# Late steps of a hybrid decoder kernel moved, and its paged key scores spread into the next stage

## The chip, the cores and the metric

The kernel runs on one core of one Trainium2 chip. The metric is device time in microseconds (us). The kernel before takes 2168.29 us, the median of three runs (2164.63 to 2173.03).

## The reference, cut to what matters

One layer of a decoder works on a prompt (1024 tokens behind 16 learned meta tokens) and on a sample batch (8 sequences of 4 new tokens, each with 1024 past tokens in a paged cache). Everything is in 32-bit floating point.

```python
h = rms_norm(x, norm_pre_g)
(q, k, v), sg, (gq, gk, gv, gf), gg = branch_inputs(h, w_in, w_alpha, b_alpha)   # h @ w_in, split
o_sb  = sb_prompt(q, k, v, sb_bias)          # or sb_sample(...) with past keys and values by page_table
o_gla = gla_prompt(gq, gk, gv, gf)           # or one gla_chunk from state_gla
mixed = concat([o_sb * silu(sg), rms_norm(o_gla) * silu(gg)])
x = x + rms_norm(mixed @ w_out, norm_post_g)
```

`w_in` is 2048 x 7184 and `w_out` 2048 x 2048. The stick-breaking attention has 8 heads of 128: the weight of a key is exp(log_sigmoid(z) - the sum of softplus(z) over all later keys). The gated linear attention has 4 heads with keys of 128 and values of 256, and its decay comes from a rank of 16 (`w_alpha`). For the samples the scores of the past keys are needed: 8 sequences x 8 pages x 8 heads = 512 blocks of 128 keys, each against 4 queries.

## The kernel before, in words

All 1072 tokens (16 + 1024 + 32) stay on chip as hT, 16 tiles of 128 features, each split into a high part `hh` and a low part `hl`. `inproj` (L279) makes one block of 128 output columns: it loads the weights 256 rows at a time (`weight_chunk`, L177: one DMA on SyncE's queue, the high part cast on ScalarE, L184, the low part subtracted on VectorE, L185), and does three matmuls (high x high, high x low, low x high; L289 to L291) for each of 16 row blocks and three chunks of tokens, into three PSUM buffers `acc`. A projection is 8 weight chunks x 3 token chunks = 24 steps of six matmuls.

The order of the work is laid out by hand. `Weaver` (L51) holds a heap of Python generators, each due at a certain beat. After each of the 24 steps `inproj` calls `W.beat()`, which lets every generator that is due record its next piece; `yield n` makes it due n beats later. One beat is called a unit here. `flush` calls the beat until no generator is left but those spawned as `lasting`; `drain` until none at all is left. Beats of a flush or a drain have no projection in them. A scheduler then sets the final order on each engine from what was recorded; pieces under `urgent()` (weights, evictions of `acc`) go ahead.

The stages are these:
- The first heads' loads and norms, then 8 attention heads (`head`, V, K and Q projections), the low-rank product of the decay (`low_rank`, L297: the load `war`, the split into `wa` on ScalarE and VectorE, then 96 matmuls into `acc_ga`), and the gate projections 0 to 2.
- The gated linear attention (pool `gp`): for each of 4 heads the projections gk, gq and two of gv. `decay` (L709) loads `w_alpha` six times into 16 rows each, and for each chunk of tokens loads `ga`, does one matmul `al` (L723) and goes on to the cumulated decay `cb`. `own` (L741) makes the diagonal products P_d (L747, L753), three of them into two PSUM buffers, each multiplied by the identity on VectorE (L749, L754). `level` does seven further steps. `inside` (L794) runs `own` and the levels, then the end of the keys: `packed` (L829: a copy into `rep` on VectorE, a transpose on TensorE) and `by_token` (L839: transposes, L845, into kd). `chunks` (L888) starts when kd is there. `samples_out` (L872) scales two tiles on VectorE (L876), and transposes them (L882) three units later. Gate projections 3 and 4 follow.
- The paged stage (pool `dp`): the weights of the samples from the scores (`new_keys` L1077, `chain` L1092), the value pages (`vr`, 64 loads of 512 KB), and gate projections 5 to 13.
- The output product by seven block products: gates 14 and 15, then `step` with `weights` (L1270) for `w_out`.

**The paged keys.** `z_feed` (L344) is a lasting generator. For each page it does four products on VectorE (L379), one per query: the key page `kp` (64 KB, three buffers) times the query row `qb`, summed into a column of `zt`. It loads two pages ahead. A finished `zt` goes to memory (`zd`, L384), from where `chain` fetches it in the paged stage, once all heads of that sequence are through (`z_done`). Each page is due two units after the one before. All its tiles are in the pool `dk`, which the tiles of `weight_forms` (L395) share; `dk` closes before the paged stage, and the drain at L999 ahead of that runs the feed to its end.

SyncE issues nearly all DMAs, in order: weights, pages, states and outputs stand in one queue. The staging tiles (`stage`, 128 x 384) come from one pool `stg` of seven buffers. `W.mark` ties the first product of a page, by an order without a semaphore, behind the last projection matmul recorded.

Of the kernel before, what the change touches and what calls it, by code (L numbers as in the profile page):

```python
# [20 lines left out]
P = 128  # L21
# [29 lines left out]
class Weaver:  # L51
# [25 lines left out]
    def drain(self):  # L77
        while self.heap:
            self.beat()
# [3 lines left out]
def hybrid_step(ctx: ExitStack, tc: tile.TileContext, x_prompt, x_sample, cache_k, cache_v, state_gla,  # L83
# [213 lines left out]
    def low_rank():  # L297

        war = stage("war")
        warv = war[:, :256].rearrange("p (k c) -> p k c", c=16)  # L300
        nc.sync.dma_start(warv, w_in[0, :, C_GA:C_GA + 16].rearrange("(k p) c -> p k c", p=P))
        wa = [stg.tile([P, 8, 32], F32R, tag="stg", name=f"wa{i}") for i in range(2)]
        for i in range(2):
            act.copy(wa[i][:, :, 0:16], warv[:, 8 * i:8 * i + 8])
            vec.tensor_tensor(wa[i][:, :, 16:32], warv[:, 8 * i:8 * i + 8], wa[i][:, :, 0:16].bitcast(F32), ALU.subtract)
        acc = [accp.tile([P, 512], F32, tag="acc", name=f"acc_ga_{c}") for c in range(3)]
# [15 lines left out]

    dk_cm = tc.tile_pool(name="dk", bufs=2, side="right")
# [20 lines left out]
    def z_feed(rate):  # L344
# [8 lines left out]
        def fetch(h, b, i):  # L353
            if i == 0:
                qbs[h, b] = dk.tile([P, NT, P], F32, tag="qb", bufs=2, name=f"qb{b}_{h}")
                nc.sync.dma_start(qbs[h, b][:], qsd[b * NT:(b + 1) * NT, h * P:(h + 1) * P].partition_broadcast(P))
            kps[h, b, i] = dk.tile([P, P], F32, tag="kp", bufs=3, name=f"kp{b}_{h}_{i}")
# [5 lines left out]
        for n, (h, b, i) in enumerate(pages()):  # L363
# [10 lines left out]
            if i == 0:  # L374
                zt = dk.tile([P, NT, NPG], F32, tag="zt", name=f"zt{b}_{h}")
            kp = kps.pop((h, b, i))
            for t in range(NT):
                jk = dk.tile([P, P], F32, tag="jk", bufs=1, name=f"jk{b}_{h}_{i}_{t}")
# [60 lines left out]
    with tc.tile_pool(name="sp", bufs=1) as sp, tc.tile_pool(name="sps", bufs=1, space=PSUM) as sps:  # L439
# [195 lines left out]
    with tc.tile_pool(name="gp", bufs=1) as gp, tc.tile_pool(name="gps", bufs=1, space=PSUM) as gps:  # L635
# [73 lines left out]
        def decay(g, cb):  # L709

            raw = stage(f"walr{g}")[:96, :P]
            for i in range(6):
                nc.sync.dma_start(raw[16 * i:16 * i + 16], w_alpha[0, :, g * P:(g + 1) * P])
            wal = gp.tile([96, P], F32R, tag="wal", name=f"wal{g}")
            act.copy(wal[:], raw)
            vec.tensor_tensor(wal[64:96, :], raw[64:96], wal[64:96, :].bitcast(F32), ALU.subtract)
            for c, (lo, hi) in enumerate(CHUNKS):
                n = hi - lo
                ga = stg.tile([96, 384], F32R, tag="stg", name=f"ga{g}_{c}")
                nc.sync.dma_start(ga[:, :n].bitcast(F32), gad[:, lo:hi])  # L720
                yield 5
                ps = gps.tile([P, 512], F32, tag="P", bufs=2, name=f"al{g}_{c}")
# [18 lines left out]
        def own(g, at, kt, qt):  # L741

            for c0 in (0, EB):
                ps = gps.tile([P, 512], F32, tag="P", bufs=2, name=f"P{g}_d_{c0}")
                for i in range(4):
# [4 lines left out]
                                  ident[:].unsqueeze(1).to_broadcast([P, 4, P]), ALU.mult)  # L750
            ps = gps.tile([P, 512], F32, tag="P", bufs=2, name=f"P{g}_d_8")
# [42 lines left out]
        def inside(g, at, kt, qt, cb, res):  # L794

            own(g, at, kt, qt)
# [24 lines left out]
            packed(kt[:, REAL:T], pk[:], 2, f"k{g}")  # L821
# [7 lines left out]
        def packed(src, dst, lo, nm):  # L829
# [681 lines left out]
```

## Time and profile before

| What | us |
|---|---|
| median of three runs | 2168.29 |
| profiled execution | 2170.9 |
| its span | 2169.2 |
| TensorE busy (PE) | 2083.5 |
| VectorE busy (DVE) | 1571.3 |
| ScalarE busy (ACT) | 989.6 |
| mean granted clock of TensorE | 0.989 |

A page of the profile gives busy times by engine, groups of instructions by source line (L379 is line 379 of the kernel), and DMA queues. Views of the trace add: who waited for whom (waits), busy time in chosen windows with the granted share of TensorE's clock, and instructions in order of time (timeline). PE is the matmuls, PEld the loads of their stationary operand, SPq the queue of SyncE. Matmuls overlap in the records: one of 384 columns is shown with some 330 ns, and they follow each other at about half of that.

### The profile page before, as it was taken

What the parts mean: (1) busy time and instruction counts of PE and PEld (TensorE: products, weight loads), DVE (VectorE), ACT (ScalarE), POOL (GpSimd) and SP (SyncE); (2) the same over time, 40 slices, a digit from 0 to 9 for tenths busy, and PEclk for the clock granted to TensorE, in tenths of its full rate; (3) what the DMA queues carried; (4) which work ended last, traced back from release to release, by engine and by line L of the source; (5) the groups of instructions that cost most, each with busy time, mean ns of one, the idle gap of its engine ahead of it and who ended that gap; (6) DMA issues with size and microseconds to landing.
All of it is one profiled execution on the core that took longest, in us unless ns stands there. A gap on an engine that the chain in (4) does not pass through costs nothing.

```text
span 2169.2 us, 43319 instructions
## 1 busy us (share of the span) xinstructions
PE 2083.5 (96%) x12546; PEld 1877.2 (87%) x12546; DVE 1571.3 (72%) x6592; ACT 989.6 (46%) x2536; POOL 83.7 (4%) x298
## 2 busy tenths in 40 slices
PE   5999999999999999989999999999999999999997
PEld 5999999999999979889899898998888897777765
DVE  6368889888898889788887888877544337453575
ACT  7345546565555646323535335243443335342332
POOL 0000010100001010010000000000000000000000
PEclk9999999999999999999999999999999999999998
DMA  6225554555545444423333433334776666452484
GB/s 194 54 72 135 143 152 138 154 154 138 165 140 158 139 126 119 133 76 81 104 99 86 113 81 106 94 84 136 221 232 219 222 200 201 130 157 73 129 277 172
DMA packets 380803, 304.02 MB, mean 140 GB/s; under 512 B 50771, under 2 KB 321043, under 8 KB 380563
## 3 DMA queue, kind: packets, MB, share of 16 engines
q1 hardware_dynamic: 378370, 300.97, 47.5%
q8 instruction: 99, 1.62, 0.3%
q14 instruction: 142, 1.16, 0.2%
q10 hardware_dynamic: 2192, 0.27, 0.1%
HBM read 243.39 MB, written 57.72 MB: 139 GB/s over the span
## 4 chain that ended last, share of the span: by engine, by line
PE 67%; DVE 14%; DMA 11%; ACT 3%; issue 3%; SPq 1%; POOL 0%; DVEq 0%; ACTq 0%; POOLq 0%
DVE jk L379 5%; DMA kp<-in_cache_k_dram 5%; PE acc_g L289 4%; PE acc_g L291 4%; PE acc_g L290 4%; PE b L1420 4%; PE b L1421 4%; PE b L1422 3%; PE acc_k L289 3%; PE acc_k L290 3%; PE acc_k L291 3%; PE acc_gv L289 2%; PE acc_gv L291 2%; PE acc_gv L290 2%; PE acc_q L289 2%
## 5 line engine op out<-in xcount | busy, mean ns | idle before, releaser
L379 DVE SCALAR_TENSOR_TENSOR jk<-kp,qb 128x128 f32<-128x128 f32 x2048 | 590.9, 289 | 93.4 <-DMA kp<-in_cache_k_dram 54.0
L289 PE MATMUL acc_g<-hT,wh_g 128*128 128x384 f32 (+2 forms) x768 | 253.8, 330 | 1.4 <-ACT gx L433 1.1
L291 PE MATMUL acc_g<-hT,wl_g 128*128 128x304 f32 (+2 forms) x768 | 248.1, 323 | 0.4 <-DVE wl_g L185 0.4
L290 PE MATMUL acc_g<-hT,wh_g 128*128 128x304 f32 (+2 forms) x768 | 247.9, 323 | 0.0
L1420 PE MATMUL b<-ring,f 128*128 128x512 f32 x416 | 166.4, 402 | 7.3 <-ACT gx L433 3.5
L289 PEld LDWEIGHTS acc_g<-hT,wh_g 128*128 128x128 f32 x768 | 145.0, 189 | 27.0 <-ACT wh_g L184 13.4
L1284 DVE TENSOR_TENSOR ring<-wr,ring 128x512 fp32r<-128x512 f32 x104 | 70.7, 690 | 132.0 <-ACT ring L1283 131.7
L379 DVE DVE_READ_ACCUMULATOR jk<-kp,qb 128x1 f32 x2048 | 166.1, 81 | 0.0
L1421 PE MATMUL b<-ring,f 128*128 128x512 f32 x416 | 163.1, 392 | 1.0 <-DVE ring L1284 1.0
L1422 PE MATMUL b<-ring,f 128*128 128x512 f32 x416 | 162.8, 391 | 0.0
L291 PEld LDWEIGHTS acc_g<-hT,wl_g 128*128 128x128 f32 x768 | 144.9, 189 | 2.6 <-issue 1.9
L290 PEld LDWEIGHTS acc_g<-hT,wh_g 128*128 128x128 f32 x768 | 145.0, 189 | 0.7
L1283 ACT CAST ring<-wr 128x512 fp32r<-128x512 f32 x104 | 64.0, 621 | 161.4 <-DMA wr<-in_w_out_dram 79.8
L507 ACT ACTIVATE X<-X 127x512 f32<-127x512 f32 (+4 forms) x112 | 54.9, 491 | 166.5 <-DVE X L506 166.3
L289 PE MATMUL acc_gv<-hT,wh_gv 128*128 128x384 f32 (+1 forms) x384 | 129.9, 338 | 0.0
L289 PE MATMUL acc_k<-hT,wh_k 128*128 128x378 f32 (+1 forms) x384 | 127.6, 332 | 0.0
L291 PE MATMUL acc_gv<-hT,wl_gv 128*128 128x384 f32 (+1 forms) x384 | 126.5, 329 | 0.0
L290 PE MATMUL acc_gv<-hT,wh_gv 128*128 128x384 f32 (+1 forms) x384 | 126.2, 329 | 0.0
L290 PE MATMUL acc_k<-hT,wh_k 128*128 128x378 f32 (+1 forms) x384 | 125.4, 326 | 0.0
L289 PE MATMUL acc_q<-hT,wh_q 128*128 128x368 f32 (+2 forms) x384 | 125.3, 326 | 0.0
L291 PE MATMUL acc_k<-hT,wl_k 128*128 128x378 f32 (+1 forms) x384 | 125.2, 326 | 0.0
L290 PE MATMUL acc_q<-hT,wh_q 128*128 128x368 f32 (+2 forms) x384 | 123.6, 322 | 0.0
(427 smaller groups left out, 5488.1 us busy)
## 6 DMA issues: line engine op xcount, KB each, us to landing
kp<-in_cache_k_dram SPq DMA_DIRECT2D x512, 64.0 KB
vr<-in_cache_v_dram SPq DMA_DIRECT2D x64, 512.0 KB
qb<-qsd SPq DMA_DIRECT2D x64, 256.0 KB
tf<-in_w_out_dram SPq DMA_DIRECT2D x64, 256.0 KB
td<-tf SPq DMA_DIRECT2D x64, 256.0 KB
wr_g<-in_w_in_dram SPq DMA_DIRECT2D x128, 128.0 KB
wr<-td SPq DMA_DIRECT2D x64, 256.0 KB
wr<-in_w_out_dram SPq DMA_DIRECT2D x48, 256.0 KB
```

Source lines behind the costliest of these rows:

```text
L289: mm(acc[c][:, :n], wh[:, k2, :], hh[k][:, lo:hi], start=(k == 0), stop=False)
L290: mm(acc[c][:, :n], wh[:, k2, :], hl[k][:, lo:hi], start=False, stop=False)
L291: W.mark = mm(acc[c][:, :n], wl[:, k2, :], hh[k][:, lo:hi], start=False, stop=(k == NK - 1)).ins
L379: ins = vec.scalar_tensor_tensor(jk[:], kp[:], 1.0, qbs[h, b][:, t, :], ALU.mult, ALU.mult, accum_out=zt[:, t, NPG - 1 - i:NPG - i])
L507: act.activation(X, X, AF.Exp)
L1283: act.copy(wh, r)
L1284: vec.tensor_tensor(wl, r, wh.bitcast(F32), ALU.subtract)
L1420: mm(bk[:], ah, wh, start=first and k == 0, stop=False, skip_group_check=True)
L1421: mm(bk[:], ah, wl, start=False, stop=False, skip_group_check=True)
L1422: mm(bk[:], al, wh, start=False, stop=last and k == 7, skip_group_check=True)
```

## The change

It has two parts. The first moves instructions in the recorded order:
- the load of `war` and the split into `wa` become a generator of their own, due 58 units after the start of the last head, that is within its Q projection (`low_rank_weights`);
- `decay` waits six units between the load of `w_alpha` and its cast, and loads each chunk's `ga` ahead of the chunk that uses it;
- `own` yields three units after each of its two large products;
- the copies into `rep` are made ahead of a wait instead of just before the transpose, and the wait for the keys grows from 5 to 7 units;
- `samples_out` waits nine units instead of three;
- `new_keys` waits 10 and 2 units instead of 2 and 10;
- the first four tiles of `w_out` are loaded before gate projection 15.

The second part concerns the paged keys: every sixth page is due three units after the one before instead of two (13/6 units per page on average); the tiles of `z_feed` are in a pool `zq` of their own, which closes after the paged stage; the drain at the end of the gated stage leaves one generator, the feed, on the heap; and the paged stage ends with a drain instead of a flush.

```diff
-    def drain(self):
-        while self.heap:
+    def drain(self, keep=0):
+        while len(self.heap) > keep:
             self.beat()
...
-    def low_rank():
+    wa = []
+    def low_rank_weights():
         war = stage("war")
...
         nc.sync.dma_start(warv, w_in[0, :, C_GA:C_GA + 16].rearrange("(k p) c -> p k c", p=P))
-        wa = [stg.tile([P, 8, 32], F32R, tag="stg", name=f"wa{i}") for i in range(2)]
+        yield 6
+        wa.extend(stg.tile([P, 8, 32], F32R, tag="stg", name=f"wa{i}") for i in range(2))
...
+    zq_cm = tc.tile_pool(name="zq", bufs=2, side="right")
+    zq = zq_cm.__enter__()
     dk_cm = tc.tile_pool(name="dk", bufs=2, side="right")
...
-        W.spawn(z_feed(lambda n: 2), lasting=True)
+        W.spawn(z_feed(lambda n: 2 + (n % 6 == 5)), lasting=True)
...
         for h in range(HEADS):
+            if h == HEADS - 1:
+                W.spawn(low_rank_weights(), 58)
             head(h)
...
+            def load_ga(c):
+                lo, hi = CHUNKS[c]
+                gas[c] = stg.tile([96, 384], F32R, tag="stg", name=f"ga{g}_{c}")
+                nc.sync.dma_start(gas[c][:, :hi - lo].bitcast(F32), gad[:, lo:hi])
+
+            load_ga(0)
+            yield 6
             wal = gp.tile([96, P], F32R, tag="wal", name=f"wal{g}")
...
                 yield 5
+                ga = gas.pop(c)
+                if c < 2:
+                    load_ga(c + 1)
...
                 vec.tensor_tensor(at[:, j:j + 4, :], ps[:].rearrange("p (a t) -> p a t", t=P),
                                   ident[:].unsqueeze(1).to_broadcast([P, 4, P]), ALU.mult)
+                yield 3
...
-            own(g, at, kt, qt)
+            yield from own(g, at, kt, qt)
...
-            yield 5
+            rep_ = three(kt[:, REAL:T], f"k{g}")
+            yield 7
...
             for i in range(2):
                 vec.tensor_scalar(ow[i], ow[i], r[:, i:i + 1], None, ALU.mult)
-            yield 3
+            yield 9
...
-        W.drain()
+        W.drain(1)
...
         def new_keys():
-            yield 2
+            yield 10
...
-            yield 10
+            yield 2
...
-        W.flush()
+        W.drain()
+    zq_cm.__exit__(None, None, None)
...
+        firsts = []
+        for k in range(4):
+            firsts.append(oy.tile([P, 512], F32, tag="wr", name=f"wr10_{k}")[:])
+            spread(nc.sync.dma_start(firsts[k], w_out[0, P * k:P * (k + 1), 0:512]))
         gate_group(15)
```

In `z_feed` the tiles qb, kp, zt and jk change their pool from `dk` to `zq`; in `gv_tok` the copy `three(...)` moves ahead of `yield 2`; `weights` takes its first four tiles from `firsts`.

More of the change, by code (lines that the diff above doesn't have):

```diff
@@ L817, in inside @@
             vec.tensor_tensor(kt[:, :T], kt[:, :T], ke[:, :T], ALU.mult)
-            yield 5
+            rep_ = three(kt[:, REAL:T], f"k{g}")
+            yield 7
             kd = xtile(f"kd{g}")
             pk = gp.tile([96, P], F32R, tag="pk", name=f"pk{g}")
-            packed(kt[:, REAL:T], pk[:], 2, f"k{g}")
+            packed(rep_, pk[:], 2, f"k{g}")
             by_token(kt, kd, (0, 4), col, f"k{g}")
@@ L827, in inside, with three, packed @@
             res["kd"], res["ebl"], res["pk"] = kd, ebl, pk
-        def packed(src, dst, lo, nm):
-            ps = gps.tile([P, 512], F32, tag="tr", name=f"trp_{nm}")
+        def three(src, nm):
             rep = stage(f"rep_{nm}")[:, :96]
             vec.tensor_copy(rep.rearrange("p (a t) -> p a t", a=3), src.unsqueeze(1).to_broadcast([P, 3, NSMP]))
+            return rep
+        def packed(rep, dst, lo, nm):
+            ps = gps.tile([P, 512], F32, tag="tr", name=f"trp_{nm}")
             nc.tensor.transpose(ps[:96, :P], rep, ident[:])
@@ L852, in gv_tok @@
         def gv_tok(g, f, c, lo, raw, v, pv):
+            if c == 2:
+                rep = three(raw[:, REAL - lo:T - lo], f"v{g}_{f}")
             yield 2
@@ L855, in gv_tok @@
             if c == 2:
-                packed(raw[:, REAL - lo:T - lo], pv[:, f * P:(f + 1) * P], 1, f"v{g}_{f}")
+                packed(rep, pv[:, f * P:(f + 1) * P], 1, f"v{g}_{f}")
         def chunk_out(g, c, rows, ow, ssq):
```

27 lines of the change are left out of this document (15 added, 12 removed).

## The prediction

> **What bounds the kernel now.** I read the page first. The span and the busy line say that TensorE (PE) is the engine to follow:
>
> ```profile
> span 2169.2 us, 43319 instructions
> ...
> PE 2083.5 (96%) x12546; PEld 1877.2 (87%) x12546; DVE 1571.3 (72%) x6592; ACT 989.6 (46%) x2536; POOL 83.7 (4%) x298
> ```
>
> PE is idle for 2169.2 - 2083.5 = 85.7 us. The change adds and removes no matmul, so it can only win idle time of PE, and time in which PE runs at a lower clock. Next comes the view of PE's waits, in which the idle time has names:
>
> ```profile
> PE otr_s L882 <- DVE ow_s L876: 7.1, 4, 2.9
> PE P_d L753 <- DVE at L749: 6.6, 3, 5.6
> ...
> PE acc_ga L310 <- DVE q L616: 3.6, 1, 3.6
> PE b L1420 <- ACT gx L433: 3.5, 2, 3.0
> PE al L723 <- DMA kp<-in_cache_k_dram: 3.4, 1, 3.4
> ...
> PE Cs L1080 <- issue: 2.7, 1, 2.7
> PE tr_k L845 <- DVE pk L837: 2.7, 4, 0.8
> ...
> PE acc_gk L289 <- ACT gx L433: 1.9, 1, 1.9
> ```
>
> The columns are the total in us, the number of waits and the longest. All are single waits at seams of the recorded order, not a steady shortage. The third view is busy time and granted clock in short windows around the larger of them:
>
> ```profile
> 786.00:796.00 10.00, 6.62 (x35) 3.95 (x36) 8.95 (x43) 4.33 (x15) 0.21 (x1) 0.83 0.62 191
> 898.00:908.00 10.00, 8.14 (x41) 7.82 (x40) 5.85 (x30) 3.77 (x10) 0.00 (x0) 0.83 0.48 141
> 912.00:932.00 20.00, 15.39 (x77) 14.86 (x76) 13.71 (x74) 6.54 (x15) 9.96 (x34) 0.83 0.40 101
> 964.00:976.00 12.00, 8.28 (x35) 8.19 (x36) 8.94 (x44) 0.81 (x2) 0.00 (x0) 0.72 0.26 67
> 1090.00:1098.00 8.00, 5.83 (x38) 5.38 (x37) 5.27 (x36) 1.63 (x7) 0.00 (x0) 1.00 0.31 83
> 1224.00:1232.00 8.00, 6.20 (x40) 5.75 (x39) 4.88 (x35) 1.59 (x7) 0.00 (x0) 1.00 0.41 109
> 1360.00:1368.00 8.00, 5.21 (x24) 5.12 (x25) 5.12 (x35) 1.57 (x6) 0.00 (x0) 0.79 0.22 55
> 1522.00:1536.00 14.00, 11.26 (x51) 9.97 (x51) 9.77 (x29) 8.30 (x21) 0.00 (x0) 0.76 0.71 214
> 1812.00:1822.00 10.00, 6.60 (x20) 4.54 (x21) 10.00 (x21) 5.89 (x13) 0.11 (x1) 0.83 0.67 210
> ```
>
> The columns are the window, its length, the busy times of PE, PEld, DVE, ACT and POOL, the granted clock, the DMA share and GB/s. Behind most gaps the clock falls too, so a gap costs more than its length. I count (1 - clock) x length as lost beside the gap: 1.7 us at 786, 1.7 at 898, 3.4 at 912, 3.4 at 964, 1.7 at 1360, 3.4 at 1522, 1.7 at 1812.
>
> The last views are those of the stages, because the change moves VectorE (DVE) work between them. The rows are the attention stage, the gated stage and a stretch of the paged stage:
>
> ```profile
> 217.00:760.00 543.00, 537.81 (x3232) 510.43 (x3233) 478.47 (x2227) 306.57 (x785) 44.19 (x149) 1.00 0.52 148
> 901.00:1505.00 604.00, 579.49 (x3796) 541.46 (x3796) 495.60 (x2571) 241.86 (x712) 11.83 (x41) 0.98 0.37 97
> 1530.00:1740.00 210.00, 209.76 (x1370) 178.71 (x1369) 93.53 (x223) 84.32 (x194) 0.00 (x0) 0.99 0.70 224
> ```
>
> PE's idle time is 5.2 us in the first, 24.5 us in the second and 0.2 us in the third. DVE is busy 88%, 82% and 45%. The paged stage is already full on PE: nothing can be won inside it, only lost.
>
> **The late instructions.** "Unit" is one call of the beat, that is six projection matmuls. L289 runs twice per unit, so the next row gives 120 / 99 = 1.21 us per unit in the paged stage:
>
> ```profile
> 1560.00:1680.00 120.00, 65.47 (x198) 36.97 (x197) 1.00 0.70 225
> ```
>
> In the gated stage, 432 units (18 projections of 24) lie in about 604 us: 1.4 us each. Seven places are moved, each worth its gap plus its clock:
>
> 1. The low-rank product, 3.6 + 1.7 = 5.3 us. The view names the q eviction. ACT's timeline shows why it was late: it stood behind two casts of V, which had to wait for their loads.
>
> ```profile
> 787.57 0.51 ACT L478 CAST V<-vr 127x384 fp32r<-127x384 f32 x1 [0.83 <-DMA vr<-out_dram]
> 787.98 0.85 ACT L615 ACTIVATE q<-acc_q 128x368 fp32r<-128x368 f32 x2
> ```
>
> With `war` and `wa` done in the projection before, the changed order issues the last V load ahead of the weight load wr_g_2, where it stood behind wr_g_4. But ACT now has three V casts ahead of the first q eviction instead of two. I credit 4.5.
>
> 2. `decay`, 3.4 + 3.4 = 6.8 us. `al` comes six units later (8 us), and its `ga` is loaded one chunk ahead. The longest wait was 3.4 us. I credit 6.
>
> 3. `own`, 6.6 + 3.4 = 10.0 us. Three units (4.2 us) now lie between the three diagonal products, which share two PSUM buffers. The longest wait was 5.6 us, so some may stay. I credit 8.5.
>
> 4. `samples_out`, 7.1 + 1.7 = 8.8 us; six units (8 us) against a longest wait of 2.9. I credit 7.5.
>
> 5. `tr_k`, 2.7 us in four waits of at most 0.8; two units, and the copy into `rep` stands ahead of them. I credit 2.
>
> 6. `new_keys`, 2.7 + 3.4 = 6.1 us; eight units (10 us). But in the changed DVE order its operand `nones` stands directly ahead of wl_g_4, and waits for POOL, so a late POOL would now stop a weight. I credit 3.5.
>
> 7. The start of the output product, 3.5 + 1.7 = 5.2 us. PE waits for a gate eviction that stands on ACT behind casts of f. With the first four w_out loads ahead of gate 15, the changed order has that eviction behind the cast of s_5 instead of s_6; the next eviction still stands behind s_6. I credit 3.5.
>
> Together: 44.9 us at stake, 35.5 credited. Each place is bounded by nothing won and its full price. What could be lost is a chain that now ends too late. In the gated stage three edits push the same chain: own 6 units, the wait before `packed` 2, and the level steps with them. The keys' last transpose then ends exactly with the last unit of the second gv projection, and the chunks start four units (5.6 us) later instead of twelve. I charge 4 us for such new waits, between 0 and 15. The stage ring of seven buffers is held longer by `ga` and by the two `ow`; that is in the same 4 us.
>
> **The pages.** One page is four products on DVE, each with a read of the accumulator:
>
> ```profile
> L379 DVE SCALAR_TENSOR_TENSOR jk<-kp,qb 128x128 f32<-128x128 f32 x2048 | 590.9, 289 | 93.4 <-DMA kp<-in_cache_k_dram 54.0 <-DMA qb<-qsd 2.2 <-DVE at L785 0.6
> L379 DVE DVE_READ_ACCUMULATOR jk<-kp,qb 128x1 f32 x2048 | 166.1, 81 | 0.0
> ```
>
> Their union in the attention stage is the next row: 1650 records are 206 pages, 1.19 us each; end to end the two instructions would be 1.48. I take 1.3.
>
> ```profile
> 217.00:760.00 543.00, 244.62 (x1650) 0.00 (x0) 1.00 0.52 148
> ```
>
> Counting the yields, the feed starts at unit 57 and the gated stage ends at unit 1072. At two units per page the 512th page falls in unit 1079, and the drain adds 9 empty units. At 13/6 units per page the last falls in unit 1164: about 44 pages move into the first 92 units of the paged stage. The drain keeps the feed alone and adds none.
>
> What is won ahead of that is small: DVE has 8% fewer pages in its way, against 5.2 us of idle PE in the attention stage. I take 1 us (0 to 4). What is paid comes in the paged stage: 92 units are some 108 us. The DVE work that is there now takes 45% of it, 48 us, and 44 pages take 57 us. That is 105 of 108: **DVE has no room left**, so each wait for a key page goes almost straight to PE. The trace has these waits in the attention and the gated stage:
>
> ```profile
> DVE jk L379 <- DMA kp<-in_cache_k_dram: 15.1, 16, 2.9
> ```
> ```profile
> DVE jk L379 <- DMA kp<-in_cache_k_dram: 28.4, 20, 3.5
> ```
>
> That is 0.07 us per page in the first (206 pages) and 0.13 in the second (217). The paged stage has a DMA share of 0.70 instead of 0.52 and 0.37, so I take 0.3 us per page: 13 us, of which the weights that DVE has made ahead absorb about half. I add 3 us for gate evictions that wait for DVE, as the 1.9 us at 901 did. Charge: 10 us, bounds 0 and the second rival's price. The scores themselves are not late: batch 0 is complete at unit 1060 and asked for at 1080; every later batch has more room (17 units per batch against 24).
>
> **Sum.** 35.5 + 1 - 4 - 10 = 22.5 us won. The profiled execution took 2170.9 us (its span and 1.7 us around it), so 2148.4 for such a one. The median of the runs is 2.6 us below it: 2145.8, rounded to **2146**.
>
> **A rule on the clock.** A gap of 1.9 us, at 901, was followed by a clock of 0.83, and gaps of about 2 us, at 1093 and 1228, left it at 1.00. The Trainium skill, page "TensorE: Matmul & The Clock Gate", section "HAM oscillation — how this bites in real kernels", says that the clock is throttled by idle gaps over about 3.4 us. By that rule the clock losses behind the gaps of at most 3.0 us would not be theirs, and 6.8 us of what is at stake (places 4, 6 and 7) would not come back; of the credit they are some 4.5 us, and the time would be 2150. The row at 898 speaks against the rule, so I keep them.
>
> **The rivals.**
> - *The gaps come back elsewhere.* DVE, ACT and SP run in order, and in the gated stage DVE is busy 82%; an instruction that PE meets later can find the same engine late again, above all where places 3 and 5 use up the cover ahead of the chunks. Half the credit (18) and the 14 us charged leave 5 us: 2164. For it: three moves on one chain. Against it: the waits are short (0.8 to 5.6 us) against 2.8 to 10 us of added distance.
> - *DVE becomes the bound in the paged stage, and the kernel is slower.* Nearly all transfers are in one hardware queue, and a value page is eight times a key page:
>
> ```profile
> q1 hardware_dynamic: 378370, 300.97, 47.5%
> ...
> kp<-in_cache_k_dram SPq DMA_DIRECT2D x512, 64.0 KB
> vr<-in_cache_v_dram SPq DMA_DIRECT2D x64, 512.0 KB
> ```
>
> At 224 GB/s one value page occupies the DMA engines for 2.3 us. The feed loads two pages ahead, 5.2 us. If a key page stands behind a value page or two, the wait can be 1.4 us per page: 62 us on a DVE with 3 us to spare. PE would lose about 55 us, against 32.5 us won elsewhere: 2168 + 22 = 2190. It decides from about 0.9 us per page. The Trainium skill, page "DMA: Bandwidth & Descriptors", section "Queues, rings and completion order", speaks for it: descriptors on one engine's ring are consumed in order. Against it: PE and the weights have slack of several us in that stage, and no wait of PE for `vr` is in the trace.
> - *All credited in full, DVE keeps up:* 44.9 + 4 - 3 is 46 us, 2122.
>
> **How the numbers follow.** Forecast (2128 to 2157) 0.58, full gain 0.10, gaps come back 0.15, DVE bound 0.17. A measurement of this kernel can tell about 0.5% (11 us) from no change. So faster by more: 0.58 + 0.10 = 0.68; within: 0.15; slower: 0.17. The range is 2120 to 2184: from the full gain to the second rival, whose far part, a tenth, is left out.
>
> **What would show it.** PE's waits for otr_s, P_d, acc_ga, al and Cs should be gone or under 1 us each, and the windows in which the clock fell should be at 1.00. In the first 110 us of the paged stage, DVE should be busy over 90%, and PE idle for under 10 us; `jk` waiting for `kp` by more than 0.9 us per page there would make the prediction wrong, as would new waits of PE for kd, U or P in the gated stage.

## The result, and the profile after

The changed kernel takes 2174.51 us (median of 22 runs, 2167.98 to 2180.53) where the kernel before takes 2167.15 us in the same series (22 runs). The ratio is 1.0034, with a 95% interval of 1.0023 to 1.0044: about 7 us slower, where 22.5 us of gain were forecast. The profiled execution after has a span of 2172.7 us against 2169.2. That of before (2170.9 us) lies 3.7 us above the median of its series, so a difference of a few us between two profiles is not a finding.

The head of the page after, busy time by engine:

```profile
span 2172.7 us, 43317 instructions
...
PE 2089.5 (96%) x12546; PEld 1875.4 (86%) x12546; DVE 1573.0 (72%) x6592; ACT 994.1 (46%) x2536; POOL 84.6 (4%) x298
```

PE is idle for 83.2 us instead of 85.7: hardly any idle time went away, so it must have moved. The view of PE's waits after (engine, line, tile, what it waited for: total us, times, longest) tells where to. Line numbers are those of the changed kernel: vr and dO are L1095, the paged product jk is L387, the paged loads are L345.

```profile
PE dO L1095 <- DMA vr<-in_cache_v_dram: 11.2, 9, 2.2
PE acc_g L290 <- ACT gx L441: 5.5, 3, 3.1
PE C L1136 <- ACT ds_h L1057: 3.6, 4, 2.7
...
PE acc_gk L290 <- ACT gx L441: 3.1, 1, 3.1
PE b L1456 <- ACT b L1355: 3.1, 2, 2.4
...
PE tr_k L871 <- DVE pk L863: 2.7, 4, 0.7
...
PE acc_ga L316 <- ACT qsm L626: 1.8, 1, 1.8
...
PE al L743 <- DMA wr_gq<-in_w_in_dram: 1.2, 1, 1.2
```

otr_s, P_d and Cs, 16.4 us before, are gone from the list; acc_ga and al are down to under 2 us each. In their place stand 11.2 us for value pages, a wait that the list of before doesn't have, and waits for gate evictions. All of these but acc_gk, b, tr_k, acc_ga, al and the longest one of acc_g (3.1 us, in gate 15) lie in the paged stage.

The 16 gate projections are good milestones: a gate is 144 matmuls into acc_g, and the start of its first one can be read from the records. In us:

| Kernel | start to gate 3 | gate 3 to output product | output product | span |
|---|---|---|---|---|
| before | 1430.3 | 384.6 | 354.3 | 2169.2 |
| after | 1405.1 | 417.0 | 350.6 | 2172.7 |
| difference | -25.2 | +32.4 | -3.7 | +3.5 |

Up to gate 3 the changed kernel wins 25.2 us, close to the 28.5 + 1 - 4 = 25.5 forecast for that part, and in the stage with the paged keys it loses 32.4. Windows cut at gates 6, 7, 8, 9 and 10 of the changed kernel show the stretch that loses (window, length, busy PE, PEld, DVE, ACT, POOL with their counts, granted clock, DMA share, GB/s):

```profile
1507.50:1536.80 29.30, 29.30 (x189) 24.32 (x188) 18.73 (x84) 10.42 (x25) 0.00 (x0) 1.00 0.72 230
1536.80:1577.10 40.30, 34.62 (x196) 25.71 (x192) 23.84 (x116) 11.60 (x26) 0.00 (x0) 0.96 0.67 191
1577.10:1617.60 40.50, 34.24 (x195) 26.46 (x193) 23.64 (x115) 11.48 (x26) 0.00 (x0) 0.96 0.60 185
1617.60:1654.80 37.20, 33.34 (x197) 26.50 (x193) 17.06 (x63) 11.52 (x26) 0.00 (x0) 0.95 0.74 226
1654.80:1684.00 29.20, 29.20 (x197) 24.81 (x193) 15.70 (x37) 14.30 (x33) 0.00 (x0) 1.00 0.81 251
```

About as many matmuls (197 and 196) take 29.2 us in the last row, without pages, and 40.3 us in the second. And yet **DVE is busy 59% of that row** (23.84 of 40.30), not over 90%, and the DMA share is lower than in the last row. Neither the engine nor the transfers are full; something is late. The first 110 us of the paged stage, for which the prediction had named its signs, give the same picture: DVE is busy 65%, not over 90%, and PE is idle for 11.9 us, not under 10:

```profile
1475.00:1585.00 110.00, 98.13 (x562) 80.06 (x560) 71.78 (x356) 35.31 (x84) 0.72 (x3) 0.95 0.63 183
```

What is late is seen in the waits of the changed kernel between 1507 and 1655 us:

```profile
ACT gs L428 <- DVE gs L427: 36.6, 7, 12.4
...
DVE jk L387 <- DMA kp<-in_cache_k_dram: 28.4, 19, 4.4
...
PE dO L1095 <- DMA vr<-in_cache_v_dram: 11.2, 9, 2.2
```

and, for the queue of SyncE, in the same window:

```profile
SPq L181 <- DVE wl_g L186: 24.7, 16, 3.8
```

DVE waits for key pages, SyncE waits for DVE before it may load the next weights into a buffer (and so keeps the pages behind them in its queue waiting), ACT waits for DVE in the gate's silu (and keeps later evictions of acc_g behind it), and PE waits for value pages and for ACT. A stretch of the timeline shows how it goes. First SyncE's issues (start, length, instruction):

```profile
1537.15 0.47 SPq L364 DMA_DIRECT2D qb<-qsd  x1
1538.41 0.35 SPq L345 DMA_DIRECT2D kp<-in_cache_k_dram  x1
1539.59 0.35 SPq L345 DMA_DIRECT2D vr<-in_cache_v_dram  x1
1540.77 0.33 SPq L345 DMA_DIRECT2D kp<-in_cache_k_dram  x1
1541.20 0.38 SPq L392 DMA_DIRECT2D zd<-zt  x1
1542.41 0.33 SPq L345 DMA_DIRECT2D vr<-in_cache_v_dram  x1
```

then the other engines behind it:

```profile
1541.84 0.32 PE L292 MATMUL acc_g<-hT,wl_g 128*128 128x368 f32 x1
1543.19 0.29 DVE L387 SCALAR_TENSOR_TENSOR jk<-kp,qb 128x128 f32<-128x128 f32 x1 [4.31 <-DMA kp<-in_cache_k_dram]
...
1544.40 1.05 PE L1095 MATMUL dO<-vr,dA 128*32 128x512 f32 x4 [2.24 <-DMA vr<-in_cache_v_dram]
...
1545.87 0.29 DVE L387 SCALAR_TENSOR_TENSOR jk<-kp,qb 128x128 f32<-128x128 f32 x1 [1.37 <-DMA kp<-in_cache_k_dram]
...
1547.14 1.92 PE L1095 MATMUL dO<-vr,dA 128*32 128x512 f32 x4 [1.69 <-DMA vr<-in_cache_v_dram]
...
1549.00 0.69 PE L290 MATMUL acc_g<-hT,wh_g 128*128 128x384 f32 x1
```

Paged issues in a row start 1.18 us apart, key and value pages in turn, and each page is used as soon as it has come. The projection stands still from 1542.2 to 1549.0. Where the 1.18 us come from, the records of the look-up (L338) and of the issue (L345) between 1507 and 1655 us tell (count, shortest, median and longest ns):

```profile
L338 SPq TENSOR_LOAD <-pt x61: 262/269/625, 1516.2 to 1651.8; - x61
L338 SPq FUSED_REGOPS  x61: 152/152/159, 1516.8 to 1652.2; - x61
...
L345 SPq DMA_DIRECT2D vr<-in_cache_v_dram x36: 332/340/836, 1508.0 to 1652.6; - x36
...
L345 SPq DMA_DIRECT2D kp<-in_cache_k_dram x30: 332/333/1843, 1520.2 to 1621.6; - x30
```

61 look-ups at 1.18 us are 72 us of SyncE's 148 (an estimate from the spacing), beside the waits for DVE. That is a price that the prediction had nowhere.

### The profile page after: what moved, and what is told of

Read it like the earlier page. It is cut to its first block, busy times and chain, and to the rows that moved or that the text cites. A ratio compares the mean times of both kernels' runs of the same rounds, so it can differ in the third digit from the quotient of the medians.

```text
span 2172.7 us, 43317 instructions
## 1 busy us (share of the span) xinstructions
PE 2089.5 (96%) x12546; PEld 1875.4 (86%) x12546; DVE 1573.0 (72%) x6592; ACT 994.1 (46%) x2536; POOL 84.6 (4%) x298
## 4 chain that ended last, share of the span: by engine, by line
PE 70%; DVE 12%; DMA 9%; ACT 4%; issue 3%; SPq 2%; POOL 0%; DVEq 0%; ACTq 0%; POOLq 0%
DVE jk L387 4%; PE b L1456 4%; PE b L1457 4%; PE b L1458 4%; PE acc_g L290 3%; PE acc_g L291 3%; PE acc_g L292 3%; DMA kp<-in_cache_k_dram 3%; PE acc_k L290 3%; PE acc_k L291 3%; PE acc_k L292 3%; PE acc_gv L290 2%; PE acc_gv L291 2%; PE acc_gv L292 2%; PE acc_v L290 2%
## 5 line engine op out<-in xcount | busy, mean ns | idle before, releaser
L387 DVE SCALAR_TENSOR_TENSOR jk<-kp,qb 128x128 f32<-128x128 f32 x2048 | 591.3, 289 | 108.4 <-DMA kp<-in_cache_k_dram 68.9
L290 PE MATMUL acc_g<-hT,wh_g 128*128 128x384 f32 (+2 forms) x768 | 257.0, 335 | 5.6 <-ACT gx L441 5.5
L292 PE MATMUL acc_g<-hT,wl_g 128*128 128x384 f32 (+2 forms) x768 | 250.5, 326 | 0.0
L291 PE MATMUL acc_g<-hT,wh_g 128*128 128x384 f32 (+2 forms) x768 | 250.4, 326 | 0.0
L290 PEld LDWEIGHTS acc_g<-hT,wh_g 128*128 128x128 f32 x768 | 147.2, 192 | 35.3 <-issue 17.7
L387 DVE DVE_READ_ACCUMULATOR jk<-kp,qb 128x1 f32 x2048 | 166.0, 81 | 0.0
L291 PEld LDWEIGHTS acc_g<-hT,wh_g 128*128 128x128 f32 x768 | 147.3, 192 | 0.7
```

What stands on the lines that cost most here:

```text
L290: mm(acc[c][:, :n], wh[:, k2, :], hh[k][:, lo:hi], start=(k == 0), stop=False)
L291: mm(acc[c][:, :n], wh[:, k2, :], hl[k][:, lo:hi], start=False, stop=False)
L292: W.mark = mm(acc[c][:, :n], wl[:, k2, :], hh[k][:, lo:hi], start=False, stop=(k == NK - 1)).ins
L387: ins = vec.scalar_tensor_tensor(jk[:], kp[:], 1.0, qbs[h, b][:, t, :], ALU.mult, ALU.mult, accum_out=zt[:, t, NPG - 1 - i:NPG - i])
```

## The experiments

Two runs first tell which part of the change the loss belongs to. The next ones ask what in SyncE's queue makes the pages late: the order (theory A: a page's load stands behind weight loads that wait for DVE, and three key tiles are too few to cover that) or SyncE's own time for look-ups and issues (theory B). The last four put A and B together as **theory Q** against **theory D**: DVE's products (57 us by the prediction) are what the stage has no room for. The DMA queue of the second rival comes up on the way. Where an expectation has a sum of 147.4 us for four gates, these are the gates from 1507.5 to 1654.8 us, 6 to 9 counted from 0. In the expectations that don't name theory Q, "gates 5 to 8" are these four and "gates 6 to 8" the three slow ones among them, 7 to 9; all else counts from 0. "Stage" below is the time from gate 3 to the output product: 384.6 us before, 417.0 after. It is read from one profile of each kernel. Where nothing else is said the diff is against the changed kernel.

### The moves alone

```diff
-        W.spawn(z_feed(lambda n: 2 + (n % 6 == 5)), lasting=True)
+        W.spawn(z_feed(lambda n: 2), lasting=True)
...
-        W.drain(1)
+        W.drain()
```

> The first part of the change alone: pages every two units and the full drain ahead of the paged stage, as before; all late instructions moved as in the change. Both theories of the loss (order of the SyncE queue, issue time of SyncE) put it on the pages that run on, so both expect the gain at the end of the gated stage to stay: gate 3 starts 25.2 us earlier in the change than before (1405.1 against 1430.3), and here 20 to 25 us earlier, a paged stage with 29 us per gate as before, and a time 20 to 30 us under that of before (2138 to 2148). If the moves themselves cost the paged stage something, gates 6 to 8 take over 32 us here too.

Measured: 2145.26 us (2142.99 to 2147.12) against 2164.23; ratio 0.9917 [0.9891, 0.9943]. Start to gate 3 1413.0 us, stage 381.0, span 2145.1. PE is never idle in the stretch that loses (window as above):

```profile
1507.00:1655.00 148.00, 148.00 (x975) 127.91 (x974) 67.52 (x160) 60.38 (x138) 0.00 (x0) 1.00 0.70 224
```

So the moves win some 19 us by themselves (24.1 between the two profiled spans), and the whole loss belongs to the pages: 417.0 - 381.0 = 36.0 us in the stage. The time is as expected; gate 3 starts 17.3 us earlier than before, less than the 20 to 25 expected. In the same window SyncE has 43 look-ups instead of 61:

```profile
L338 SPq TENSOR_LOAD <-pt x43: 262/270/864, 1507.9 to 1654.2; - x43
```

Its wait for wl_g is 34.6 us here, longer than the 24.7 of the changed kernel, and PE loses nothing by it. So that wait is no sign of the loss by itself. What the moves left in place or made new stands in PE's waits from 217 to 1420 us:

```profile
PE al L743 <- DMA kp<-in_cache_k_dram: 4.4, 1, 4.4
PE acc_ga L316 <- DVE q L624: 3.5, 1, 3.5
PE trp_v L860 <- ACT gv L876: 3.4, 1, 3.4
PE tr_k L871 <- DVE pk L863: 3.0, 4, 0.7
```

### The pages alone

The kernel before, with the rate, the pool and the drains of the change (the four tiles of `z_feed` from `zq`):

```diff
-        W.spawn(z_feed(lambda n: 2), lasting=True)
+        W.spawn(z_feed(lambda n: 2 + (n % 6 == 5)), lasting=True)
...
-        W.drain()
+        W.drain(1)
...
-        W.flush()
+        W.drain()
+    zq_cm.__exit__(None, None, None)
```

> The second part alone: the kernel before with pages every 13/6 units, their own pool, and the drain that leaves the feed. If the pages alone make the loss, gates 6 to 8 take 37 to 40 us each as in the change instead of 29, the gated stage gains under 4 us, and the time is 25 to 35 us over that of before. If the loss needs the moved instructions as well, it is within 10 us of before.

Measured: 2181.47 us (2179.82 to 2184.91); ratio 1.0086 [1.0057, 1.0115]. Start to gate 3 1412.4 us, stage 415.0. The stage is about as long without the moves, so the loss doesn't need them; against its own counterpart it is 415.0 - 384.6 = 30.4 us here and 36.0 us with the moves. But the slower pages win 17.9 us ahead of gate 3 (1430.3 to 1412.4), far more than the 1 us of the prediction and the 4 us of this expectation, and the time is 17 us over that of before, between the two cases expected.

### More key pages ahead

```diff
-            kps[h, b, i] = zq.tile([P, P], F32, tag="kp", bufs=3, ...)
+            kps[h, b, i] = deep[1].tile([P, P], F32, tag="kp", bufs=deep[0], ...)
...
-            while fetched < n + 3:
+            while fetched < n + deep[0]:
...
+        deep[:] = [8, dp]
```

`deep` is `[3, zq]` until the paged stage begins.

> The change, with eight key page buffers and eight pages loaded ahead in the paged stage instead of three. Theory A (order of the queue: a key page load stands in SyncE's queue behind a weight load that waits for VectorE, which waits for the key page): with five more pages ahead the circle is cut, VectorE's 33 us of waits for kp in 1475 to 1640 go under 8, and gates 6 to 8 return to 29 to 31 us, a time of 2138 to 2148. Theory B (issue time: SyncE executes some 31 us of instructions per gate of 29 us in this stretch): the pages are only issued earlier, the value pages later; gates 6 to 8 still add up to 8 us or more over 87, and the waits for vr grow beyond 11 us.

Measured: 2173.01 us (2170.79 to 2178.81); ratio 1.0041 [1.0026, 1.0055]; stage 415.4. Waits from 1507 to 1655 us:

```profile
PE dO L1097 <- DMA vr<-in_cache_v_dram: 11.5, 9, 2.0
...
DVE jk L388 <- DMA kp<-in_cache_k_dram: 5.5, 3, 2.6
```

DVE's wait for keys falls from 28.4 to 5.5 us, ACT's wait for DVE (gs) from 36.6 to 9.9, and the stage is 1.6 us shorter, no more than two profiles can differ by. The wait that looked like the cause, and that the prediction had named as its test, was not what bound the stage: PE's wait for vr stayed. Theory A's forecast failed; theory B's held.

### Key pages without a look-up

```diff
-            page_dma(kps[h, b, i][:], cache_k, b, i, slice(h, h + 1))
+            if (h * NB + b) * NPG + i < 464:
+                page_dma(kps[h, b, i][:], cache_k, b, i, slice(h, h + 1))
+            else:
+                nc.sync.dma_start(kps[h, b, i][:], cache_k[0, 0:1, :, h:h + 1, :].rearrange("o p h d -> p (o h d)"))
```

> The change, with the last 48 key pages (from page 464 on) read from page 0 of the cache instead of the page of the table; so the table look-up, its register load and the register arithmetic on SyncE are left out for them, about 0.75 us each, and the scores of those pages are not the reference's. Transfers, buffers and products stay. Theory B: SyncE has 8 us less to do per gate, and gates 6 to 8 go back to 29 to 32 us each. Theory A: the queue keeps its order and its waits, and gates 6 to 8 stay over 35 us each.

Measured: 2154.34 us (2149.98 to 2157.59); ratio 0.9959 [0.9943, 0.9975]; stage 400.5. As many loads of as many bytes in the same queue, and 16.5 of the 36.0 us are back. Gates 7 to 9 take 37.8, 34.3 and 31.1 us: neither all back at 29 to 32 nor all over 35, so neither theory alone forecast it. PE's waits from 1507 to 1655 us no longer have vr; a gate eviction is left, behind DVE:

```profile
PE acc_g L290 <- ACT gx L444: 7.0, 2, 5.4
```

### Both

The two edits above together.

> No look-up for the last 48 key pages (they read page 0, so their scores are not the reference's) and eight buffers in the paged stage, together. Without the look-up alone gates 5 to 8 took 133.5 us, with eight buffers alone 148.5, without any page 115.9. If issue time and the order of the queue are two halves of one loss, the two together leave 116 to 122 us and a time of 2136 to 2145. If the rest of the loss is VectorE's products standing ahead of the gates' work, it stays near 133.

Measured: 2151.05 us (2146.53 to 2151.91); ratio 0.9935 [0.9915, 0.9956]; stage 392.2. In the profiled stage the eight tiles, worth 1.6 us alone, are worth 8.3 more once the look-ups are gone; 24.8 of 36.0 us are back. By the medians they are worth 3.3 us (2154.34 against 2151.05) and the two intervals overlap, so the size is open. Gates 6 to 9 take 125.6 us and the time is over 2145: the two together leave more than expected. The window, beside that of the moves alone above:

```profile
1507.00:1655.00 148.00, 144.91 (x910) 118.76 (x910) 95.04 (x403) 55.95 (x126) 0.00 (x0) 1.00 0.75 229
```

### No loads, all the products

```diff
-            while fetched < n + 3:
+            while fetched < min(n + 3, 464):
...
-            kp = kps.pop((h, b, i))
+            if n < 464:
+                kp = kps.pop((h, b, i))
```

The query rows are still loaded for each sequence.

> The changed kernel, but the last 48 pages of keys are neither looked up nor loaded: DVE makes the same products from the last key tile that was loaded (so the last 48 pages' scores aren't the reference's). All of DVE's work is still in the paged stage, and SyncE has none of the pages'. Theory Q (what costs is SyncE's time for the look-ups and the order in which it issues): gates 6 to 9 come back from 147.4 us to 116 to 121, and the time is 2140 to 2150 us. Theory D (DVE's 4 products per page cost it, whenever the keys come): gates 6 to 9 stay over 130 us and the time over 2157. In the run with eight tiles and no look-up they were 125.6 us.

### All the loads, no products

```diff
+            if n >= 464:
+                vec.tensor_copy(zt[:, :, NPG - 1 - i], kp[:, :NT])
-            for t in range(NT):
+            for t in range(NT if n < 464 else 0):
```

> The changed kernel, but for the last 48 pages DVE makes one small copy from the key tile in place of the four products (so these pages' scores aren't the reference's). Look-ups, loads, buffers and DVE's wait for each key page stay. Theory Q: value pages and weights are as late as before, since SyncE does the same; gates 6 to 9 take 132 to 147 us, time 2160 to 2174, and PE still waits for vr. Theory D: DVE's 57 us are gone, gates 6 to 9 come back to 116 to 121 us and the time to 2140 to 2150. Between the two, 122 to 131 us, each has a share.

Measured: 2143.81 us (2140.36 to 2146.65), ratio 0.9908 [0.9882, 0.9933], without the loads; 2169.3 us (2166.47 to 2174.06), ratio 1.0025 [1.0013, 1.0037], without the products. The stage is 388.0 and 413.6 us: taking the loads away brings 29.0 of the 36.0 us back, taking the products away 3.4. Gates 6 to 9 are 126.4 us without the loads (a little over what theory Q said) and 143.0 without the products. From 1507 to 1655 us, first without loads, then without products:

```profile
1507.00:1655.00 148.00, 141.22 (x914) 119.78 (x913) 92.84 (x393) 54.77 (x128) 0.00 (x0) 0.98 0.67 216
```
```profile
1507.00:1655.00 148.00, 133.94 (x798) 105.99 (x797) 57.56 (x161) 48.75 (x111) 0.00 (x0) 0.98 0.68 209
```

With DVE busy for 92.84 us PE gets 914 matmuls done; with DVE at 57.56 us, 39% of the window, it gets 798. PE's waits in that window without the products name the value pages again:

```profile
PE dO L1097 <- DMA vr<-in_cache_v_dram: 9.6, 8, 2.3
```

This is the pair that settles it. Theory D falls: most of the loss comes with the loads and little with the products. It doesn't all go with the loads: 7.0 of the 36.0 us stay, and PE's waits there between 1475 and 1640 us are 4.9 us for gate evictions and 2.8 for osb.

### Three units per page

```diff
-        W.spawn(z_feed(lambda n: 2 + (n % 6 == 5)), lasting=True)
+        W.spawn(z_feed(lambda n: 3 if n >= 467 else 2 + (n % 6 == 5)), lasting=True)
```

> The change, with three units per page from page 467 on, that is in the paged stage, instead of 13/6. Per gate SyncE then has 8 key pages of 1.2 us instead of 11, some 27 us of its 29 us. Theory B (issue time of SyncE): the queue just fits, gates 5 to 8 add up to 116 to 124 us instead of 147.4 in the change, and the time is 2140 to 2152. If it is VectorE's busy share or the transfers beside the value pages, the loss is spread over more units and not smaller: 140 us or more over gates 5 to 9, a time over 2160.

Measured: 2164.94 us (2159.74 to 2172.22); ratio 1.0013 [1.0001, 1.0025]; stage 407.3. Gates 6 to 11 take 31.2, 31.8, 35.6, 35.4, 35.6 and 31.4 us: less per gate, over more gates; 9.7 of 36.0 us are back. (This profile is of the fastest of the ten runs, 5 us under their median, so it may flatter.) Theory B's forecast failed: gates 6 to 9 add up to 134.1 us, not 116 to 124, and the time is over 2160, as its rivals had it. So 8 pages per gate don't just fit into SyncE's queue; thinner spreading doesn't hide the loads.

### GpSimd issues the key pages

The diff is that of the run without look-ups, with its last line replaced (and, in the second run, the eight tiles as well):

```diff
+                pg = nc.gpsimd.value_load(pt[:1, b * NPG + i:b * NPG + i + 1], min_val=0, max_val=NPOOL - 1)
+                nc.gpsimd.dma_start(kps[h, b, i][:], cache_k[0, bass.ds(pg, 1), :, h:h + 1, :].rearrange("o p h d -> p (o h d)"))
```

> The change, with the look-up and the load of the last 48 key pages issued by GpSimd instead of SyncE, three buffers as before. SyncE's issue time and its order are both out of the way for key pages; transfers, products and their order on VectorE stay. Theory B, and theory A too, expect gates 5 to 8 at 116 to 126 us together (147.4 in the change, 116 without pages) and 2138 to 2150 us. If the loss is VectorE's (its order, its busy share) or the transfers', gates 5 to 8 stay over 133 us.

> The last 48 key pages issued by GpSimd, into eight buffers. The version that keeps everything of the change and relieves SyncE and the order: gates 5 to 8 at 116 to 122 us, and with the earlier end of the gated stage (3 to 8 us under the moves alone) 2132 to 2145 us. If it stays over 2155, the loss is not on SyncE.

Measured: 2179.95 us (2176.01 to 2183.14), ratio 1.0073 [1.0051, 1.0095], and with eight tiles 2183.37 us (2180.16 to 2192.23), ratio 1.0101 [1.0071, 1.0131]; stage 426.1 and 429.5. All forecasts of theories A and B for these two runs failed. PE has no wait for vr any more, as they say of a relieved SyncE, but the keys come no earlier, since GpSimd takes longer to issue them. Waits of the first from 1507 to 1655 us:

```profile
POOL kp L370 <- issue: 58.5, 18, 5.8
DVE jk L391 <- DMA kp<-in_cache_k_dram: 30.5, 19, 4.5
...
PE acc_g L290 <- ACT gx L445: 21.2, 4, 10.8
```

58.5 us in 18 waits that nothing in the profile explains are 3.3 us ahead of each of these issues, where SyncE needs 1.18 from one to the next. With eight tiles GpSimd is asked to issue them even earlier, ahead of its own work for ntri, and Cs waits 14.3 us for that. By its expectation the second run, at over 2155 us, would put the loss elsewhere than on SyncE; but GpSimd's own slowness came in its place, so the two runs tell of GpSimd as an issuer and nothing for or against theory D.

### Pages copied ahead and loaded by fours

```diff
+            m = (h * NB + b) * NPG + i
+            if m >= 476:
+                if m % 4 == 0:
+                    quad[0] = late_pool[0].tile([P, 4, P], F32, tag="kq", bufs=2, ...)
+                    nc.sync.dma_start(quad[0][:], pgd[:, m - 476:m - 472, :])
+                kps[h, b, i] = quad[0][:, m % 4, :]
+                return
...
+            if 240 <= n < 348 and n % 3 == 0:
+                k = (n - 240) // 3
+                page_dma(pgd[:, k, :], cache_k, 3 + (k + 4) // NPG, (k + 4) % NPG, slice(HEADS - 1, HEADS))
```

In the second run the copy is issued by GpSimd, at the same place of the program.

> The changed kernel with the whole computation, but the last 36 pages of keys are looked up and copied from DRAM to DRAM in the gated stage (one per third page there), and in the paged stage nine loads without a look-up fetch four pages each, a group ahead, into tiles of the paged stage's pool. Theory Q: SyncE is relieved in the paged stage of some 36 look-ups and 27 issues, and gates 6 to 9 take 117 to 126 us; the gated stage, where SyncE has 36 issues more in some 200 us, loses 0 to 5 us; time 2140 to 2155. Theory D: gates 6 to 9 stay over 130 us and the time over 2160.

> The run before this one (the last 36 pages copied from DRAM to DRAM in the gated stage and loaded by fours in the paged stage), with the 36 look-ups and copies issued by GpSimd at the same places of the program, where SyncE issued them. The whole computation is kept. There the fourth gate started at 1419.8 us, 14.7 us later than in the changed kernel, and the gates after it were 31.4, 30.5, 30.2 and 29.0 us long. Theory Q (SyncE's time is what costs, in the gated stage too): the fourth gate starts at 1403 to 1410 us, gates 6 to 9 stay at 119 to 125 us, and the time is 2147 to 2156 us. Rival: the transfers themselves (36 pages read and written while the weights are loaded) cost it; then the fourth gate still starts after 1415 us and the time is 2160 to 2170. Third case: GpSimd takes so long to issue that its memsets for at and gq come late; then PE has new waits in the gated stage, and the time is over 2165.

Measured: 2165.48 us (2162.56 to 2173.49), ratio 1.0012 [0.9997, 1.0026], and 2175.34 us (2171.61 to 2181.09), ratio 1.0049 [1.003, 1.0068]. In both the stage is nearly mended, 390.1 and 392.2 us, and gates 6 to 9 take 121.1 us in the first, with more bytes per second than in any other run of this stretch:

```profile
1507.00:1655.00 148.00, 141.34 (x895) 120.22 (x894) 103.26 (x465) 58.63 (x133) 0.00 (x0) 0.98 0.77 242
```

So it is not the bytes (242 GB/s here, 206 after) and not DVE's time (103.26 us here against 83.77 after). The gates of the first run are as theory Q expected (those of the second take 125.9 us, just over); the times of both are not, for the copies cost elsewhere. Issued by SyncE in the gated stage they delay gate 3 by 14.7 us (1419.8). Issued by GpSimd they don't stay there: nothing ties them to their place, GpSimd runs them at once from 44 to 136 us, and DVE and ACT wait behind it (first stage of the second run):

```profile
POOL pgd L387 <- issue: 81.4, 36, 10.9
...
DVE ntri L125 <- POOL t_ntri L123: 19.6, 1, 19.6
DVE V L501 <- ACT V L500: 18.5, 1, 18.5
ACT V L500 <- POOL vr L494: 17.8, 1, 17.8
```

Gate 0 then starts 25.6 us later than in the changed kernel, gate 3 25.3 us. So this run can't say whether SyncE's time or the transfers made the gated stage slower in the run before it; that stays open.

## Why the prediction was wrong

The sum was 35.5 + 1 - 4 - 10. Place by place:

- **The late instructions ahead of gate 3** (credited 28.5, less 4 for new waits: 24.5). The moves alone win 1430.3 - 1413.0 = 17.3 us there. otr_s and P_d went as forecast. The low-rank product (credited 4.5), `al` (6) and the copies into `rep` (2) won little or nothing: with the moves alone acc_ga waits 3.5 us (3.6 before), al 4.4 (3.4 before) and tr_k 3.0 (2.7). Only beside the slower pages did acc_ga and al fall. The new waits were of the forecast size: trp_v, 3.4 us, was the one.
- **Cs and the start of the output product** (3.5 each). The moves alone win 384.6 - 381.0 = 3.6 and 354.3 - 351.1 = 3.2, the size forecast. That the second is the work of the move isn't shown: the run of the pages alone, which doesn't have it, has 352.2 us, within the 349.9 to 353.1 of the runs that have it, and with it gate 15 has a new wait for an eviction (acc_g, 2.8 us with the moves alone, 3.1 after). All moves together were credited 35.5 - 4 = 31.5 us and won 24.1 between the spans, 19 between the medians.
- **The slower page rate ahead of the spill** (1, at most 4). Mis-sized. Without the moves it wins 17.9 us up to gate 3; beside them, nine profiles with the changed rate, and nothing else changed up to there, reach gate 3 at 1399.3 to 1405.8, against 1413.0 in the one profile of the moves alone: 7 to 14. One page in thirteen fewer ahead of DVE and SyncE removes part of the same late waits as the moves do, which the prediction gave to the moves alone: with the pages alone otr_s waits 1.6 us instead of 7.1 and P_d 3.8 instead of 6.6, though neither was moved. So it is luck that the two parts together came near the forecast 25.5 us; the one was sized too high and the other too low.
- **The pages in the paged stage** (10 us). This is the step that failed: it measured 417.0 - 381.0 = 36.0 us. The step said that DVE "has no room left" (105 of 108 us; 92 units at its own 1.21 us are 111) and that the price is DVE's wait for each key page, less what DVE has made ahead. DVE was busy 59% of the worst gates; without the products 32.6 of the 36.0 us stay, and without the loads 7.0. The prediction priced each page's products on DVE and its bytes in the queue, and left out what the page asks of SyncE: a look-up and an issue, 1.18 us, in the one in-order queue that also carries value pages and weights.
- **The second rival** had the right sign and place, but not the mechanism. It wanted a key page to stand behind value pages in the DMA queue, for 1.4 us per page, a figure that it worked out from no row. Loads of the same bytes without the look-up lose 19.5 us instead of 36.0, and loads by fours (36 of the pages) at 242 GB/s lose 9.1. With the look-ups gone and eight tiles 11.2 us stay, and 7.0 with no loads at all; if such parts add up, some 4 us is what issues and transfers together can have cost there. The sentence of the Trainium skill that was called for it (page "DMA: Bandwidth & Descriptors", section "Queues, rings and completion order") is about the order of descriptors in a ring; what cost most here is the time and order of SyncE's instructions. The rival's threshold of 0.9 us per page didn't decide either: DVE waits 24.8 us for some 32 pages in the first 110 us of the stage, 0.78 per page, and 28.4 / 30 = 0.95 from 1507 to 1655 us, but with these waits cut to 5.5 us the loss was the same.
- **The clock.** The sum counted 15.3 us of lower clock at the moved places, as if the gap brought it. With the moves alone (1 - clock) x length still adds up to 10.1 us (0.72 over 12 us at 784 and at 910, 0.76 over 7 at 990, 0.83 over 10 at 1768), of 17.0 before (the row at 898 included). Nor do gap and clock go together in the changed kernel's trace: over a gap of 3.1 us (acc_gk) the clock stayed at 1.00, and it fell in a stretch in which PE was busy for 9.54 of 10 us:

```profile
888.00:910.00 22.00, 18.88 (x118) 18.56 (x117) 16.43 (x85) 7.31 (x18) 0.20 (x1) 1.00 0.54 151
1040.00:1050.00 10.00, 9.54 (x78) 7.00 (x76) 6.59 (x38) 5.21 (x19) 0.12 (x1) 0.83 0.30 86
```

In the three slow gates it was 0.95 to 0.96, and PE's longest waits for vr in the stretch shown were 2.2 and 1.7 us, 1.05 us of products apart. The Trainium skill, page "TensorE: Matmul & The Clock Gate", section "HAM oscillation — how this bites in real kernels", warns of idle gaps over about 3.4 us. The full clock at 3.1 us agrees with it, the lower clock behind the shorter waits doesn't. What decides it, no run here separates.

Of what would show it, the moved waits did go (otr_s, P_d and Cs gone; acc_ga at 1.8 and al at 1.2 us a little over the bound), DVE over 90% and PE idle for under 10 us were wrong, and "jk waiting for kp by more than 0.9 us per page" was near its bound (0.78) without being the cause. The windows of lower clock at the low-rank product, the start of the paged stage and the output product did not go: 0.83, 0.76 and 0.83 from 786, 1496 and 1796 us after.

Shown: the loads make most of the loss (29.0 of the 36.0 us go with them, 3.4 with the products), and it is not their bytes. Of the loads' part the look-ups are the larger share (16.5 us go with them alone). The order (few tiles, so that each load stands behind weights that wait for DVE) counts only once they are gone, by 3 to 8 us. Not shown: how PE's further loss in the slow gates divides, since its records are busy for 34.62 us where they take 29.20, of which the clock accounts for 40.3 x 0.04 = 1.6. The runs without look-ups also read one page again and again, and lose the tie by which `page_dma` records each look-up behind the fourth load of that cache before it. Neither was separated from the look-up itself, though the loads by fours, which read the pages that the table names, agree with them.

The best kernel of the study is the moves alone, 2145.26 us: 0.83% faster than before. No version with pages in the paged stage beat it by more than the intervals (2143.81 us came without loading those pages).

## What to carry to other kernels

When work moves to another stage, count it on every engine that touches it, the issuing engine too: instructions per item times their spacing in the timeline, against the time in which that in-order queue isn't waiting already. A stage with low busy shares everywhere can still be full, if one queue ties several loads to each other's buffers. And a long wait is not yet the cause: take it away by itself (here with eight tiles) before it gets the blame.

## What the runs showed of the hardware

- A load from a looked-up address costs SyncE far more than its issue: 0.27 us for the register load, 0.15 and less for the address arithmetic, 0.33 for the DMA instruction, and 1.18 us from one to the next. The Trainium skill, page "DMA: Bandwidth & Descriptors", section "Latency and other measured facts", gives a floor of about 600 ns for the register load and doesn't say from which memory. The rows above, from a table on chip, have a shortest of 262 and a median of 269 ns, so by the trace it is the sequence and not this one instruction that is dear.
- GpSimd as the issuer of such loads idles 3.3 us ahead of an issue in the paged stage (58.5 us in 18 waits), nearly three times SyncE's spacing, and whatever stands behind it on GpSimd waits (17.8 us for ntri with eight tiles).
